# The first network of a hybrid decoder in block products, the last pair too, and the reciprocal root on VectorE

## The chip, the cores and the metric

One core of one Trainium2 chip runs the whole program. The metric is the device time of one execution in microseconds (us); lower is better. TensorE multiplies (PE in the views), VectorE is DVE, ScalarE is ACT, GpSimd is POOL, SyncE is SP.

## The reference

Two decoder layers work on 512 prompt tokens and 32 sample tokens (544 columns) of width 1024. Each layer has a gated network, a mixing stage and a second gated network:

```python
def swiglu(x, w_up, w_down):
    a, u = jnp.split(x @ w_up, 2, axis=-1)
    return (jax.nn.silu(a) * u) @ w_down

x = layer_norm(ALPHA * x + 0.5 * swiglu(x, p['ffn1_up'], p['ffn1_down']), p['ln1_g'], p['ln1_b'])
proj = x @ p['w_in'] + p['b_in']          # q, k, v, glu, gates
...                                       # window attention and causal convolution
c = jax.nn.silu(layer_norm(c, p['conv_ln_g'], p['conv_ln_b']))
mix = (jax.nn.sigmoid(g_attn) * (attn @ p['w_attn_out'])
       + jax.nn.sigmoid(g_conv) * (c @ p['w_conv_out']))
x = layer_norm(ALPHA * x + mix @ p['w_out'], p['ln2_g'], p['ln2_b'])
x = layer_norm(ALPHA * x + 0.5 * swiglu(x, p['ffn2_up'], p['ffn2_down']), p['ln3_g'], p['ln3_b'])
```

The inner width of the gated networks is 2816 = 11 x 256. All is float32.

## The kernel before

Activations lie with their features on the partitions and the 544 tokens along the columns, in four pieces of 256 features (a pair of 128). The columns are worked in two halves of 272, called hf 0 and hf 1. Every float32 product is made of three passes over operands that are split into a high and a low part (`split`: a cast on ScalarE, L460, and a subtraction on VectorE, L461); weights are split by `prep`-like steps in the same way (L291 on ScalarE, L292 on VectorE).

A standard unit (`unit`, L451 to L453) multiplies 256 output columns by one half of the tokens: 8 x 2 x 3 = 48 matmuls. An up pair j of a network is two weights, "a" for the gate and "u" for the value, so four units; `silu` applies the activation on ScalarE (L605) and `gated` the multiplication on VectorE (L611). The last unit of a layer's network is a down unit (`down_unit`, L717 adds its result).

Three of the four networks make the pairs j = 2 to 9 as block products instead (`up_fast`): each block of 128 columns is one 2 x 2 product by seven multiplications, which `product` (L664) does in 12 matmuls each, and one preparing matmul (L678). The left factors are differences of weight blocks (L312, L322, L352), made by a planner (`fill`, `steps`), which hands work to VectorE and ScalarE piece by piece while TensorE's estimated time advances. The right factors T are differences of blocks of the activations (`right`, L568 to L574); they are made where the norm before the network writes its result (`ln_out`). The first layer's first network has no norm in front of it. There `residual` (L585, L586) makes the scaled tokens that the result is added to, and all its pairs are standard units, in groups of 3, 3, 3 and 2 (`GROUPS`), each followed by the down units of the group before. Pair 10 is made of standard units in every network.

At the end of a network (`tail`) the last down units run beside the layer norm of the two halves: `centre` sums over the features on TensorE (L482) and subtracts the mean (L487), `newton` sums the squares (L504) and calls `rsqrt`, and `scale` spreads the result over the columns on TensorE (L512) and multiplies (L516). `rsqrt` makes three small operations on VectorE (L526 to L528) and eleven on GpSimd (L530 to L540), in series. These norms stand in 14 places; the last one of the program works on rows instead and has two more chains (L893, L902).

`setup_layer` loads the layer's small vectors by DMAs on GpSimd's queue, turns them on TensorE (L992, L1001, L1012) and copies them out of PSUM on VectorE (L994, L1002, L1013). It runs after the first two pairs (`up_first`) of the layer's first network, in `mark`. Transposed late tokens are brought in between the units of `up_first` (`late`). Weights come by DMAs on SyncE's queue (L166, L172).

The order of instructions is that of the program, apart from down units and norm steps at a network's end and in the middle of a network, which are mixed by due times.

## Time and profile before

| what | value |
|---|---|
| median of 3 runs | 2626.16 us (2626.13 to 2630.38) |
| profiled execution, its own time | 2630.69 us |
| span of the profile | 2628.7 us |
| TensorE busy | 2552.5 us (97%) |
| VectorE busy | 1715.0 us (65%) |
| ScalarE busy | 1126.2 us (43%) |
| GpSimd busy | 298.0 us (11%) |
| granted TensorE clock, mean of the run | 0.981 |

The span is the part of an execution that the profile covers; 2.0 us of the profiled execution lie outside it. Busy time is the time in which an engine worked on an instruction. A clock of 1.00 is 2.4 GHz, and 0.50 is 1.2 GHz, the lower of the two levels.

### The profile page before, as it was taken

How to read it: one execution, taken by the hardware profiler on the slowest of the kernel's cores; microseconds unless marked ns; L12 is line 12 of the kernel's file. 1: busy time of each engine (PE TensorE's matmuls, PEld its weight loads, DVE VectorE, ACT ScalarE, POOL GpSimd, SP SyncE). 2: the span in 40 equal slices, each digit the busy share in tenths (PEclk: the TensorE clock that was granted, in tenths of full speed). 3: DMA queues.
4: the chain of work that ended last, by engine and by line, in shares of the span. 5: the costliest groups of instructions: out<-in, count | busy, mean ns of one | idle time of the engine just before them, and what ended most of it. 6: DMA issues, size and time to landing. Idle time of an engine off the chain costs nothing.

```text
span 2628.7 us, 47397 instructions
## 1 busy us (share of the span) xinstructions
PE 2552.5 (97%) x20110; PEld 2502.8 (95%) x20110; DVE 1715.0 (65%) x2567; ACT 1126.2 (43%) x1972; POOL 298.0 (11%) x499
## 2 busy tenths in 40 slices
PE   8999999999999999999989999989999999999996
PEld 7999999988999999999989999989899999999996
DVE  4333237797986567666556666549979766676645
ACT  4222124477526254443344443245773353444431
POOL 2000001722301000000020000017232000000001
PEclk8999999999999999999989999989999999999998
DMA  7223133231322213332422333312214222233331
GB/s 219 83 89 104 54 109 85 50 95 53 101 65 87 91 58 96 97 97 89 133 75 82 97 97 97 116 49 76 82 53 113 69 81 87 78 93 97 97 101 39
DMA packets 302628, 232.15 MB, mean 88 GB/s; under 512 B 43812, under 2 KB 300020, under 8 KB 302320
## 3 DMA queue, kind: packets, MB, share of 16 engines
q1 hardware_dynamic: 298576, 220.37, 27.8%
q0 software_dynamic: 3840, 8.76, 1.1%
q8 instruction: 157, 2.57, 0.4%
q14 instruction: 55, 0.45, 0.1%
HBM read 225.69 MB, written 9.16 MB: 89 GB/s over the span
## 4 chain that ended last, share of the span: by engine, by line
PE 82%; DVE 8%; POOL 4%; ACT 3%; issue 2%; DMA 1%; DVEq 0%; POOLq 0%; ACTq 0%
PE pa L453 20%; PE pa L451 20%; PE pa L452 20%; PE pa L664 11%; PE pb L664 8%; DVE pr L1126 3%; POOL f L1141 2%; DVE wl L292 1%; DVE pr L461 1%; PE pb L1266 1%; DVE at L1247 1%; PE pa L1237 1%; PE pb L1278 1%; ACT at L1251 1%; PE pb L512 0%
## 5 line engine op out<-in xcount | busy, mean ns | idle before, releaser
L451 PE MATMUL pa<-pr,wh 128*128 128x272 f32 (+1 forms) x4032 | 1176.1, 293 | 18.7 <-ACT pr L460 11.1
L453 PE MATMUL pa<-pr,wl 128*128 128x272 f32 (+1 forms) x4032 | 1173.4, 292 | 4.9 <-DVE wl L292 4.9
L452 PE MATMUL pa<-pr,wh 128*128 128x272 f32 (+1 forms) x4032 | 1170.3, 291 | 3.7 <-DVE pr L461 3.6
L451 PEld LDWEIGHTS pa<-pr,wh 128*128 128x128 f32 x4032 | 765.8, 190 | 26.0 <-ACT pr L460 13.5
L452 PEld LDWEIGHTS pa<-pr,wh 128*128 128x128 f32 x4032 | 771.5, 191 | 8.2 <-DVE pr L461 6.0
L453 PEld LDWEIGHTS pa<-pr,wl 128*128 128x128 f32 x4032 | 765.6, 190 | 6.1 <-DVE wl L292 5.7
L292 DVE TENSOR_TENSOR wl<-raw,wh 128x1024 fp32r<-128x1024 f32 (+1 forms) x268 | 309.8, 1183 | 77.3 <-ACT wh L291 54.0
L1126 DVE SCALAR_TENSOR_TENSOR pr<-u,cw,pr 128x512 f32<-128x512 f32 x480 | 344.4, 764 | 2.2 <-ACT pr L1119 2.0
L291 ACT CAST wh<-raw 128x1024 fp32r<-128x1024 f32 (+1 forms) x268 | 259.9, 1009 | 159.8 <-PE pa L453 90.9
L453 PE MATMUL pa<-pr,wd 128*128 128x272 f32 x768 | 221.8, 289 | 0.0
L451 PE MATMUL pa<-pr,wd 128*128 128x272 f32 x768 | 221.4, 288 | 0.0
L452 PE MATMUL pa<-pr,wd 128*128 128x272 f32 x768 | 220.8, 288 | 0.0
L717 DVE SCALAR_TENSOR_TENSOR pr<-pa,pr 128x544 f32<-128x544 f32 (+2 forms) x152 | 109.7, 722 | 153.5 <-PE pa L453 152.7
L530 POOL TENSOR_SCALAR nw<-nw 91x3 f32<-91x3 f32 (+2 forms) x16 | 5.6, 349 | 1703.2 <-DVE nw L526 1703.2
L460 ACT CAST pr<-f 128x544 fp32r<-128x544 f32 (+1 forms) x124 | 79.7, 647 | 216.4 <-DVE f L611 116.1
L664 PE MATMUL pa<-pr,wa 128*128 128x272 f32 x1152 | 160.9, 289 | 0.0
L664 PE MATMUL pb<-pr,ws 128*128 128x272 f32 x1152 | 159.6, 288 | 0.0
L664 PEld LDWEIGHTS pa<-pr,wa 128*128 128x128 f32 x1152 | 151.4, 188 | 0.0
L664 PEld LDWEIGHTS pb<-pr,ws 128*128 128x128 f32 x1152 | 150.0, 188 | 0.0
L452 PEld LDWEIGHTS pa<-pr,wd 128*128 128x128 f32 x768 | 145.1, 189 | 0.0
L451 PEld LDWEIGHTS pa<-pr,wd 128*128 128x128 f32 x768 | 144.5, 188 | 0.0
L453 PEld LDWEIGHTS pa<-pr,wd 128*128 128x128 f32 x768 | 144.3, 188 | 0.0
(225 smaller groups left out, 3139.6 us busy)
## 6 DMA issues: line engine op xcount, KB each, us to landing
raw<-in_ffn_up_dram SPq DMA_DIRECT2D x174, 512.0 KB, 4.4
raw<-in_ffn_down_dram SPq DMA_DIRECT2D x76, 512.0 KB, 3.6
raw<-in_w_in_dram SPq DMA_DIRECT2D x72, 512.0 KB, 4.1
raw<-in_w_in_dram SPq DMA_DIRECT2D x64, 128.0 KB, 3.0
raw<-in_w_attn_out_dram SPq DMA_DIRECT2D x32, 256.0 KB, 4.0
raw<-in_w_conv_out_dram SPq DMA_DIRECT2D x16, 512.0 KB, 3.4
raw<-in_w_out_dram SPq DMA_DIRECT2D x16, 512.0 KB, 4.3
raw<-in_ffn_down_dram SPq DMA_DIRECT2D x24, 256.0 KB, 2.8
```

What stands on the lines that cost most here:

```text
L291: ins = self.nc.scalar.copy(wh, t)
L292: self.nc.vector.tensor_tensor(wl, t, wh.bitcast(F32), op=ALU.subtract)
L451: pin(self.nc.tensor.matmul(o, lhsT=wh, rhs=h, start=k == 0, stop=False))
L452: pin(self.nc.tensor.matmul(o, lhsT=wh, rhs=lo, start=False, stop=False))
L453: pin(self.nc.tensor.matmul(o, lhsT=wl, rhs=h, start=False, stop=k == kk - 1))
L460: pin(self.nc.scalar.copy(hi, src))
L461: pin(self.nc.vector.tensor_tensor(lo, src, hi.bitcast(F32), op=ALU.subtract))
L664: mm = lambda a, b, first=False, last=False: pin(nc.tensor.matmul(o, lhsT=a, rhs=b, start=first, stop=last, skip_group_check=True))
L717: pin(nc.vector.scalar_tensor_tensor(Y[p][:, :, hs], ps, 0.5, Y[p][:, :, hs], op0=ALU.mult, op1=ALU.add))
L1126: self.last["cw"] = nc.vector.scalar_tensor_tensor(cc[:, m, 0:SEQ], u[:, m, k:k + SEQ], cw[:, 8 * k + c:8 * k + c + 1], cc[:, m, 0:SEQ], o ...
L1141: nc.gpsimd.tensor_tensor(pr[:, 4 * b:4 * b + 4, :], win, wv.unsqueeze(1).to_broadcast([128, DS, KC]), op=ALU.mult)
L1237: nc.tensor.matmul(s[:, 2 * r + t, :], lhsT=q, rhs=k, start=t == 0 and ps == 0, stop=ps == 2, skip_group_check=True)
```

## The change

Four things change.

1. The first layer's first network makes its pairs j = 2 to 9 as block products, as the others do. Its right factors are made by `first_right` from the raw tokens, in `up_first`, between the units of the second half. The function also adds the two parts of the tokens (y), which `scaled` then multiplies on ScalarE; `residual` is no longer called there.
2. Pair 10 is made as two blocks, s(10, 0) and s(10, 1), in all four networks; the weights of the last down group come through the planner.
3. The eleven operations of `rsqrt` that ran on GpSimd run on VectorE.
4. `setup_layer` issues its DMAs before `up_first`, and does the turning on TensorE in a function `turn` that is called behind `up_first`; the copies of the caches (`shift_caches`) follow it.

```diff
-        g = self.nc.gpsimd
+        g = self.nc.vector
         g.tensor_scalar_mul(u, v, RS_B * RS_B)
...
-        return o + [("a", 10), ("u", 10)] + [("dn", 4, p, 0) for p in range(4)]
+        return o + [s(10, 0), s(10, 1)] + [("dn", 4, p, 0) for p in range(4)]
...
-                    if hf and j and self.is_fast(l, f):
+                    if hf and j:
                         begin()
+                    elif hf and not Y0:
+                        first_right()
                     gated(ws[2 * j + 1], hs[j], hf, sa)
...
+        def first_right():
+
+            for xh, xl in X:
+                y = self.pair()
+                nc.vector.tensor_tensor(y, xh.bitcast(F32), xl.bitcast(F32), op=ALU.add)
+                Y0.append(y)
+                T.append(self.right(y)())
...
-            self.stop = self.pi + len(self.ffn_order(l, f)) - 10
+            self.stop = self.pi + len(self.ffn_order(l, f)) - 4
...
-            for kind, *k in self.fast_order()[4:-6]:
+            for kind, *k in self.fast_order()[4:-4]:
...
+        gl = len(GROUPF) - 1
+        turn = self.mark(l, f)
+        up_first()
+        Y += self.scaled(Y0)
+        turn()
+        middle()
+        if last:
+            self.cut = FB[FK[1][0]][0]
+        ws = []
+
+        def pre(hf):
+            if hf == 0:
+                ws.extend(self.V(l, f, "dn", gl, p) for p in range(4))
+            else:
+                self.ahead(A3)
...
-            if l == 0:
-                self.setup2()
-            self.setup_layer(l)
-            if l:
-                self.shift_caches(l)
+
+        if f != "ffn1":
+            return lambda: None
+        if l == 0:
+            self.setup2()
+        turn = self.setup_layer(l)
+
+        def rest():
+            turn()
+            self.shift_caches(l)
+        return rest
```

`right(y)` is the function that makes the factors: three differences on VectorE, a cast on ScalarE, and, when its result is called, the low part on VectorE.

**VectorE at the start.** In the rows of before, L611 multiplies a gated unit (f), L461 makes the low part of its split, L586 scales the tokens and L292 makes low parts of weights:

```order
L611 TENSOR_TENSOR f_397<-pa_416,f_397 128x544
L461 TENSOR_TENSOR pr_210<-f_397,pr_209 128x2x272
L586 SCALAR_TENSOR_TENSOR pr_674<-pr_87,pr_674 128x1088
L586 SCALAR_TENSOR_TENSOR pr_677<-pr_89,pr_677 128x1088
...
L586 SCALAR_TENSOR_TENSOR pr_683<-pr_93,pr_683 128x1088
L292 TENSOR_TENSOR wl_742<-raw_737,wh_741 128x1024
...
L611 TENSOR_TENSOR f_517<-pa_519,f_517 128x544
...
L461 TENSOR_TENSOR pr_208<-f_517,pr_207 128x2x272
...
L611 TENSOR_TENSOR f_620<-pa_622,f_620 128x544
L461 TENSOR_TENSOR pr_210<-f_620,pr_209 128x2x272
```

In the rows of the change, L592 and L442 are that multiplication and split, L620 is the addition, L549 to L555 are `right`, and L298 makes the low part of the first down weight (wd). The units are numbered up to the eighth, which is f_696:

```order
L592 TENSOR_TENSOR f_433<-pa_452,f_433 128x544
L442 TENSOR_TENSOR pr_246<-f_433,pr_245 128x2x272
L620 TENSOR_TENSOR pr_555<-pr_86,pr_87 128x1088
L549 TENSOR_TENSOR pr_557<-pr_555 128x544
L550 TENSOR_TENSOR pr_557<-pr_555,pr_557 128x272
...
L555 TENSOR_TENSOR pr_559<-pr_557,pr_558 128x1088
...
L620 TENSOR_TENSOR pr_585<-pr_92,pr_93 128x1088
...
L592 TENSOR_TENSOR f_696<-pa_733,f_696 128x544
...
L555 TENSOR_TENSOR pr_589<-pr_587,pr_588 128x1088
L442 TENSOR_TENSOR pr_246<-f_696,pr_245 128x2x272
L298 TENSOR_TENSOR wd_708<-raw_698,wd_707 128x1024
```

The four scalings have gone from VectorE, and 20 operations of `first_right` stand in their place; the eighth unit's split and the first down weight's low part stand behind them.

**TensorE at the end of the first network, first half.** In the rows of before, L504 are the sums of `newton`, L512 those of `scale`, and the rest are rows of down units:

```order
L504 MATMUL pb_3996<-ones,pr_3679 91x1 x3
L451 MATMUL pa_4105<-pr_3206,wh_3733 128x272
...
L453 MATMUL pa_4105<-pr_3206,wl_3734 128x272
...
L453 MATMUL pa_4131<-pr_3676,wl_3740 128x272
...
L453 MATMUL pa_4158<-pr_3206,wl_3746 128x272
L512 MATMUL pb_4042<-ident,nw_4001 128x91 x3
L451 MATMUL pa_4158<-pr_3676,wh_3745 128x272
```

In the rows of the change, L485 is `newton`, L493 is `scale`, and L463 is `centre` of the second half:

```order
L433 MATMUL pa_4376<-pr_3754,wd_4013 128x272
L434 MATMUL pa_4376<-pr_3753,wd_4014 128x272
L485 MATMUL pb_4277<-ones,pr_4004 91x1 x3
L493 MATMUL pb_4326<-ident,nw_4282 128x91 x3
L463 MATMUL pb_4461<-pr_4003,ones 128x272
L432 MATMUL pa_4435<-pr_86,wh_4176 128x272
```

Before, 51 rows of down units lie between the two steps; now the one follows the other. In the second half there are 84 rows between them now, and 44 before; at the second layer's first end 85, and 39 before.

**VectorE in the second half of the convolution's norm, first layer.** In the rows of before, L500 is the last sum of squares, L526 to L528 are VectorE's part of `rsqrt`; the splits L461 and the scalings L586 of the tokens follow:

```order
L500 TENSOR_TENSOR pr_8277<-pr_8277 128x272
L526 TENSOR_SCALAR nw_8657<-pb_8653 91x3
L527 TENSOR_SCALAR nw_8659<-nw_8657 91x3
L528 TENSOR_SCALAR nw_8658<-nw_8659 91x3
L461 TENSOR_TENSOR pr_8857<-pr_4717,pr_8856 128x2x272
...
L461 TENSOR_TENSOR pr_8875<-pr_7207,pr_8874 128x2x272
L586 SCALAR_TENSOR_TENSOR pr_8880<-pr_87,pr_8880 128x1088
```

In the rows of the change, L507 to L521 are `rsqrt`, L442 the splits and L567 the scalings:

```order
L481 TENSOR_TENSOR pr_8480<-pr_8480 128x272
L507 TENSOR_SCALAR nw_8860<-pb_8856 91x3
L508 TENSOR_SCALAR nw_8862<-nw_8860 91x3
...
L442 TENSOR_TENSOR pr_9060<-pr_4920,pr_9059 128x2x272
L513 TENSOR_TENSOR nw_8862<-nw_8862,nw_8860 91x3
...
L442 TENSOR_TENSOR pr_9078<-pr_7410,pr_9077 128x2x272
...
L518 TENSOR_SCALAR nw_8860<-nw_8862 91x3
L567 SCALAR_TENSOR_TENSOR pr_9083<-pr_87,pr_9083 128x1088
...
L521 TENSOR_TENSOR nw_8861<-nw_8861,nw_8860 91x3
L567 SCALAR_TENSOR_TENSOR pr_9092<-pr_93,pr_9092 128x1088
```

The fourteen operations of `rsqrt` now share the queue with four splits and three scalings. On TensorE 89 rows lie between `newton` and `scale` there, where 47 lay before.

## Rows read from the trace of the kernel before

**Rows 1.** The page: busy time and share; the chain that ended last.
```profile
PE 2552.5 (97%) x20110; PEld 2502.8 (95%) x20110; DVE 1715.0 (65%) x2567; ACT 1126.2 (43%) x1972; POOL 298.0 (11%) x499
...
PE 82%; DVE 8%; POOL 4%; ACT 3%; issue 2%; DMA 1%; DVEq 0%; POOLq 0%; ACTq 0%
```

**Rows 2.** Windows: span, busy us (count) PE, PEld, DVE, ACT, POOL; PEclk, DMA, GB/s.
```profile
60.00:395.00 335.00, 335.00 (x2666) 334.83 (x2665) 111.05 (x129) 76.51 (x96) 0.00 (x0) 1.00 0.29 91
395.00:470.00 75.00, 71.71 (x571) 70.78 (x570) 46.64 (x71) 34.56 (x56) 12.60 (x23) 1.00 0.28 75
960.00:1240.00 280.00, 280.00 (x2221) 280.00 (x2220) 195.58 (x256) 122.33 (x189) 0.00 (x0) 0.99 0.30 91
1295.00:1350.00 55.00, 45.21 (x324) 43.74 (x323) 35.16 (x56) 23.25 (x37) 9.85 (x32) 0.84 0.34 112
1690.00:1765.00 75.00, 64.78 (x483) 63.30 (x481) 41.33 (x64) 32.04 (x52) 7.85 (x23) 0.91 0.26 67
```

**Rows 3.** Groups by line and shape: busy us, mean ns, idle before, releaser.
```profile
L312 DVE TENSOR_TENSOR wd<-raw,wd 128x1024 fp32r<-128x1024 f32 x48 | 58.2, 1217 | 5.5 <-PE pa L664 2.9 <-ACT wd L322 2.6
...
L574 DVE TENSOR_TENSOR pr<-pr,pr 128x1088 fp32r<-128x1088 f32 x12 | 15.5, 1293 | 12.8 <-ACT pr L571 12.8
...
L568 DVE TENSOR_TENSOR pr<-pr 128x544 f32<-128x544 f32 x12 | 8.6, 717 | 0.0
...
L569 DVE TENSOR_TENSOR pr<-pr,pr 128x272 f32<-128x272 f32 x12 | 5.2, 437 | 0.2
```

**Rows 4.** The start, timeline (start, us, engine, what, idle before, releaser) and window.
```profile
50.73 0.72 DVE L461 TENSOR_TENSOR pr<-f,pr 128x544 fp32r<-128x544 f32 x1 [0.71 <-ACT pr L460]
51.74 4.90 DVE L586 SCALAR_TENSOR_TENSOR pr<-pr,pr 128x1088 f32<-128x1088 f32 x4 [0.29 <-ACT pr L585]
...
73.36 0.72 DVE L611 TENSOR_TENSOR f<-pa,f 128x544 f32<-128x544 f32 x1 [3.89 <-PE pa L453]
...
33.98 0.56 PE L451 MATMUL pa<-pr,wh 128*128 128x272 f32 x1 [4.22 <-DVE pr L461]
...
34.00:39.00 5.00, 5.00 (x23) 5.00 (x24) 2.57 (x6) 1.58 (x4) 0.00 (x0) 0.52 0.81 276
```

**Rows 5.** Timeline of a root's chain and scaling; two of layer two.
```profile
1315.84 0.16 DVE L527 TENSOR_SCALAR nw<-nw 91x3 int32<-91x3 int32 x1
...
1316.11 0.17 DVE L528 TENSOR_SCALAR nw<-nw 91x3 int32<-91x3 int32 x1
...
1318.84 0.19 POOL L540 TENSOR_TENSOR nw<-nw,nw 91x3 f32<-91x3 f32 x1
...
1319.08 1.58 PE L512 MATMUL pb<-ident,nw 91*128 91x91 f32 x6 [4.33 <-POOL nw L540]
...
1714.87 1.38 PE L512 MATMUL pb<-ident,nw 91*128 91x91 f32 x5 [4.54 <-POOL nw L540]
...
1739.48 0.79 PE L512 MATMUL pb<-ident,nw 91*128 91x91 f32 x5 [1.60 <-POOL nw L540]
```

**Rows 6.** Timeline of the convolution norm's second chain; a window behind it.
```profile
819.15 0.16 DVE L526 TENSOR_SCALAR nw<-pb 91x3 f32<-91x3 f32 x1 [1.10 <-PE pb L504]
...
822.54 1.23 POOL L535 TENSOR_TENSOR nw<-nw 91x3 f32<-91x3 f32 x1
...
827.07 1.40 PE L512 MATMUL pb<-ident,nw 91*128 91x91 f32 x6 [2.04 <-POOL nw L540]
...
827.00:832.00 5.00, 4.93 (x27) 4.93 (x28) 3.50 (x5) 4.97 (x9) 0.01 (x1) 0.66 0.00 0
```

**Rows 7.** Timeline of the second layer's setup; GpSimd's last early issue.
```profile
1381.64 0.38 PE L1012 MATMUL pb<-nw,f 4*128 4x4 f32 x2 [2.97 <-DVE vec L994]
...
24.16 0.55 POOL L1025 DMA_DIRECT2D out_new_conv_sample_dram<-in_state_conv_dram  x1
```

**Rows 8.** Timeline of VectorE at the end.
```profile
2613.96 2.47 DVE L893 SCALAR_TENSOR_TENSOR at<-at,mv,at 128x1024 f32<-128x1024 f32 x2
2618.76 2.74 DVE L902 SCALAR_TENSOR_TENSOR at<-at,nw,at 128x512 f32<-128x512 f32 x4 [2.32 <-POOL nw L540]
```

More of the change, by code (lines that the diff above doesn't have):

```diff
@@ L226, in plan @@
         self.tp = self.ta = self.td = 0.0
-    @staticmethod
-    def is_fast(l, f):
-        return (l, f) != (0, "ffn1")
     def ffn_order(self, l, f):
         o = []
-        if self.is_fast(l, f):
-            for kind, *k in self.fast_order():
-                if kind != "dn" or k[2] == 0:
-                    o.append((kind, *k[:2]))
-            return o
-        for g, n in enumerate(GROUPS):
-            for i in range(n):
-                o += [("a", 3 * g + i), ("u", 3 * g + i)]
-                if i == 0 and g > 0:
-                    o += [("dn", g - 1, p) for p in range(4)]
-        o += [("dn", len(GROUPS) - 1, p) for p in range(4)]
+        for kind, *k in self.fast_order():
+            if kind != "dn" or k[2] == 0:
+                o.append((kind, *k[:2]))
         return o
@@ L430, in W @@
         return ms, kk
-    def P(self, *key):
-        self.ahead(2)
-        return self.W(*key, la=1)
     def unit(self, w, xs, hf, pin=lambda i: i):
@@ L617, in new_h @@
             return h
-        def up(g, i):
-            j = 3 * g + i
-            w = self.W(l, f, "a", j, la=LAU if j < 9 else LAV)
-            sa = [silu(w, hf) for hf in range(2)]
-            w = self.W(l, f, "u", j, la=LAU if j < 9 else LAV)
-            h = new_h(g)
-            for hf in range(2):
-                gated(w, h, hf, sa[hf])
         def up_first():
@@ L717, in down_unit @@
             pin(nc.vector.scalar_tensor_tensor(Y[p][:, :, hs], ps, 0.5, Y[p][:, :, hs], op0=ALU.mult, op1=ALU.add))
-        def down(g, get=self.W):
-            for p in range(4):
-                w = get(l, f, "dn", g, p)
-                for hf in range(2):
-                    down_unit(w, g, p, hf)
-            del H[g]
         def middle():
@@ L990, in setup_layer @@
                             a["b_in"][l, DQ:].rearrange("(c p) -> c p", p=128))
[L991 to L995 removed]
         wr = a["conv_dw_w"][l].rearrange("k (c p) -> (k c) p", p=128)
[L997 removed]
+        wrows = self.f1(shape=[128, 2, 128])
         for h in range(2):
[L999 to L1001 removed]
@@ L1002, in setup_layer @@
-        self.after(nc.vector.tensor_copy(cw, ps[:, :248]), "cw")
+            nc.gpsimd.dma_start(wrows[:124, h, :], wr[124 * h:124 * h + 124, :])
         nsk = t([128, NH], F32, f"nsk{l}")
         nc.gpsimd.dma_start(nsk, a["attn_sinks"][l:l + 1, :].to_broadcast([128, NH]))
-        nc.vector.tensor_scalar_mul(nsk, nsk, -1.0)
-        nsks = t([128, 4], F32, f"nsks{l}")
-        sk4 = self.sp.tile([128, 4], F32, tag="nw", name=self.nm("nw"))
+        sk4 = self.sp.tile([128, 4], F32, tag="sk", name=self.nm("sk"))
@@ L1017, in setup_layer, with turn @@
-        self.cw.append(cw)
-        self.nsk.append(nsk)
-        self.nsks.append(nsks)
-        self.bv.append(bv)
+        def turn():
+            ps = self.p1()
+            nc.tensor.transpose(ps[:, :NVEC], rows[:NVEC, :], self.ident[:NVEC, :NVEC])
+            vec = t([128, NVEC], F32, f"vec{l}")
+            nc.vector.tensor_copy(vec, ps[:, :NVEC])
+            cw = t([128, KC * 8], F32, "cw")
+            ps = self.p1()
+            for h in range(2):
+                nc.tensor.transpose(ps[:, 124 * h:124 * h + 124], wrows[:124, h, :], self.ident[:124, :124])
+            self.after(nc.vector.tensor_copy(cw, ps[:, :248]), "cw")
+            nc.vector.tensor_scalar_mul(nsk, nsk, -1.0)
+            nsks = t([128, 4], F32, f"nsks{l}")
+            ps = self.p1()
+            nc.tensor.matmul(ps[:, :4], lhsT=sel, rhs=sk4[:4], start=True, stop=True)
+            nc.vector.tensor_copy(nsks, ps[:, :4])
+            self.vec.append(vec)
+            self.cw.append(cw)
+            self.nsk.append(nsk)
+            self.nsks.append(nsks)
+            self.bv.append(bv)
@@ L1022, in shift_caches @@
+        return turn
     def shift_caches(self, l):
```

68 lines of the change are left out of this document (2 added, 66 removed).

## The prediction

> **What bounds the kernel now.** I read the page first, then windows by stage, then the timeline around each gap of TensorE. TensorE is busy for 2552.5 of 2628.7 us and makes up 82% of the chain that ended last [rows 1], so the time is TensorE's matmuls, plus the few places where it stands. Between 60 and 395 us, in the first network, 2666 matmuls fill 335 us without a hole: 335/2666 = 0.1257 us for each [rows 2]. Block products are no dearer: 280/2221 = 0.1261 between 960 and 1240 us, in a network that has them [rows 2]. So I count matmuls at 0.1257 us and call what is left of a stretch its loss. At the end of the first network (395 to 470 us) that is 75 - 571 x 0.1257 = 3.2 us. At the ends of two networks that already work in blocks it is 55 - 324 x 0.1257 = 14.3 us (1295 to 1350) and 75 - 483 x 0.1257 = 14.3 us (1690 to 1765) [rows 2]. The reader is to see there that the networks in block products are gapless inside (280.00 of 280 us, VectorE busy for 195.58 of them) and lose time only at their ends.
>
> **Matmuls saved.** A pair of up columns as standard units is 4 units of 48 = 192 matmuls; as two blocks it is 2 x (7 x 12 + 1) = 170. Twelve pairs change: eight of the first network and the last pair of all four networks. 12 x 22 = 264 matmuls, and 264 x 0.1257 = **33.2 us** less. It holds in full only if no new block waits for its factors.
>
> **The start.** The right factors are made on VectorE between the up units of the first two pairs: for each of four pieces an addition, one difference of 0.72, two of 0.44, and the low part of 1.29 behind a ScalarE cast, for which VectorE idles 12.8/12 = 1.07 us [rows 3]. The addition of two 128x1088 tensors has no row; by the low part, of the same size and two inputs, it is 1.29. That makes 5.25 us a piece, 21.0 in all, in place of four scalings of 4.90 together [rows 4]. VectorE is free at 50.73 + 0.72 = 51.45 us. Three pieces (15.75), a multiplication and a split of a gated unit (1.44), and the fourth piece up to its cast (2.89) take it to 71.5. The eighth unit's product comes at 73.36 [rows 4]. Behind it stand, in VectorE's order, the multiplication (0.72), two small copies (0.6 by estimate: 272 columns take 0.44), the last low part (1.29), the split (0.72) and the first low part of a down weight (1.22): 77.9 us, and more if a ScalarE cast comes late [rows 3, 4]. TensorE, which before went straight on, wants this weight some 0.7 us after the unit, with only three small jobs ahead: it stands 4 us or a little more; I take 4.4. Then the clock: before, after a stand of 4.22 us, TensorE did 23 matmuls in 5 us at a granted clock of 0.52, the lower level, in place of 23 x 0.1257 = 2.9 us [rows 4]; 2.1 us more. Together **+6.5**; bounds 0 (VectorE has caught up) and 10 (a second wait behind it).
>
> **The first network's end.** Before, 51 rows of the down units lie between the norm's statistics and its scaling, and hide the reciprocal root. After, there are none in the first half, as in the other networks, whose ends lose 14.3 us. Less what the root's move gives there (below), 12.0, against 3.2 now: **+8.8**; bounds 0 and 11.1.
>
> **The root's chain.** Where nothing was beside it, the second of its 14 operations started at 1315.84 us and the last at 1318.84, and the scaling matmuls stood 4.33 us for it [rows 5]. A GpSimd operation there takes 0.19 us, but 1.23 while VectorE runs its long ones [rows 6]. On VectorE two dependent small operations start 0.27 us apart though each takes 0.17 [rows 5], so 14 of them take about 3.5 us: bare, the move is worth 0.2 us. What it gains is the stretching, and the cover that the new order puts before the scaling. In the convolution's norm the second chain ran from 819.15 until the scaling matmuls at 827.07, 7.9 us in place of 3.5; TensorE stood 2.04 us for it, and then did 27 matmuls in 5 us: 5 - 0.07 - 3.4 = 1.5 lost to the clock, 3.6 in all, twice [rows 6]. After, four splits (0.72) and three scalings (1.22) [rows 4] stand between its operations on VectorE: 3.5 + 2.9 + 3.7, less what overlaps about 9.5 us. But 89 rows of matmuls lie in the gap in place of 47, 11.2 us, so it is covered. I leave 1.0 each for what those rows no longer cover elsewhere: 2 x 2.6 = **-5.2**; bounds 0 and -7.2. At the second layer's first end the stand of 4.54 is for a stretched chain and becomes 0.7 shorter; the second, 1.60, gets 85 rows in place of 39 and goes [rows 5]: **-2.3**. The first layer's second network: **-0.2**. In the last norm the chain's first three operations (0.5 us) stood ahead of two long ones of VectorE, 2.47 us, and the scaling then waited 2.32 us for the rest on GpSimd [rows 8]; in series 3.5 + 2.5 takes the place of 0.5 + 4.8: **+0.7**, with the first of the two chains **+0.9**.
>
> The row that prices a small VectorE operation is weighed against a page. The Trainium skill, "VectorE: DVE Perf Modes", section "The TRN2 errata", gives a float32 tensor_tensor (N+151)/0.96 ns, 0.16 us here; by that figure alone, as an estimate, a chain would take 2.2 us and every exposed chain would give 1.3 more. The rows agree on the duration and not on the distance. The same page of the Trainium skill, section "The DRAIN you can't avoid" lets the next operation start only when the pipeline is empty: chained or not, so 11 operations more are 11 such distances; the trace agrees (0.27). On GpSimd's stretched rows the trace agrees with the Trainium skill, "SBUF — State Buffer", section "Who interferes with whom": a VectorE instruction with two SBUF inputs contends with GpSimd's reads.
>
> **Last pair and setup.** The two blocks of the last pair are prepared inside the blocks before them, and the last group's down weights follow inside the second. VectorE has 30% of its time free in such a stretch [rows 2]; I cost them at nothing. If the second block were late, that is a few us in each of four networks (a rival, below). At the second layer's setup TensorE stood 2.97 us behind a copy from PSUM that weight operations held up on VectorE [rows 7]; in the new order the copy comes directly: about 1.1 left, **-1.9**. The setup's small DMAs move ahead of the first units, and the cache copies behind them. They are on GpSimd's queue, which before had issued them all by 24.7 us and then idled [rows 7]; what they bring is wanted at 74 us, so neither they nor what they pass costs anything.
>
> **Sum.** -33.2 + 6.5 + 8.8 - 5.2 - 2.3 - 0.2 + 0.9 - 1.9 = **-26.6 us**. The profiled execution had 2630.7, which gives 2604.1. It lies 4.5 above the median of 2626.2, which gives **2600**.
>
> **Rivals.**
> - *The ends and the start stay hidden.* VectorE catches up in the start, and the first network's end loses no more than now: -33.2 - 9.6 + 0.9 = -41.9, 2584. For it speaks that VectorE is idle in pieces of 4 us in the start [rows 4]; against it, the orders.
> - *VectorE's queue is late in more places.* The norms keep their stands (0 in place of -5.2), the start costs 10, the end 11.1: -26.6 + 5.2 + 3.5 + 2.3 = -15.6, 2611. For it: eleven operations in 16 chains now wait their turn among operations of 0.7 to 1.3 us, in an order fixed beforehand.
> - *The root is cheaper than I count.* If the operations followed each other at their own 0.17 us [rows 5], a chain would take 2.4 us, and six exposed ends (the first halves of three networks, the last norm's two chains and one more) would give 1.1 each: -33.2, 2593. Against it stands the distance of 0.27 between two VectorE rows. The formula of the Trainium skill, "VectorE: DVE Perf Modes", "The TRN2 errata", would make it so.
> - *The other side: blocks wait for VectorE.* Each of 24 new blocks adds splits and differences to VectorE. If each made TensorE wait 26.6/24 = 1.1 us, nothing would be left; at 1.5 us the time would be 2626.2 - 26.6 + 36 = 2636. Against it stands the gapless stretch of 280 us with the same blocks [rows 2]. In the first network VectorE has nothing more to do than there.
>
> **How the numbers follow.** The forecast has 0.48, with a range of its own of 2593 to 2606. Hidden start and ends: 0.12. Late queue: 0.24. Cheap root: 0.09. Blocks that wait: 0.07, of which half is on the wrong side of no change. 0.2% is 5.3 us, about what can be told here. Faster 0.91, same 0.05, slower 0.04. The range, 2586 to 2614, takes in the cheap root and the late queue, and leaves out the two outer cases.
>
> **What would show it.** TensorE's matmuls: 264 fewer. In 60 to 400 us no gap. A stand of 4 to 5 us near 74 us with the lower clock behind it; if there is none, the first rival holds. At the first network's end a stand of about 4 us before the scaling matmuls in its first half. No stand before the scaling in the second half of the convolution's norm; if it is there with VectorE as releaser, the late queue is right. Wrong altogether if the blocks of the first network show waits for VectorE, or the loss at its end is well over 14 us.

## The result, and the profile after

The changed kernel takes 2599.26 us (median of 5 runs) against 2630.38 for the kernel before on the same chip: a ratio of 0.9888, 95% interval 0.9872 to 0.9904. Four of its runs lie between 2594.78 and 2602.92; the fifth took 3064.55 at a mean granted clock of 0.745, where the others had 0.934 to 0.982, and is left out of the ratio. The forecast of 2600 and its range held. The change itself was forecast as -26.6 and came as -31.1 by the medians: the level was met because the median of three runs before, from which it was taken, lay 4.2 us below that of five. The profiled execution took 2602.92 us with a span of 2600.8; the span is 27.9 us shorter than before.

The page of the changed kernel: busy time of each engine, then the chain that ended last.

```profile
PE 2522.6 (97%) x19846; PEld 2471.7 (95%) x19846; DVE 1882.3 (72%) x2955; ACT 1195.6 (46%) x2116; POOL 238.7 (9%) x323
...
PE 84%; DVE 8%; ACT 4%; POOL 2%; issue 1%; DMA 0%; DVEq 0%; ACTq 0%; POOLq 0%
```

Against [rows 1] TensorE has 20110 - 19846 = 264 matmuls fewer, exactly the number forecast. VectorE works 167 us more and is no bound.

Windows of the changed kernel (columns as in [rows 2]): the first network, its end, the two other ends, then three short stretches.

```profile
60.00:360.00 300.00, 296.36 (x2341) 295.63 (x2340) 211.50 (x277) 127.77 (x200) 0.00 (x0) 0.99 0.31 93
360.00:440.00 80.00, 72.02 (x547) 70.62 (x547) 53.56 (x98) 35.91 (x57) 0.15 (x1) 0.91 0.37 105
1275.00:1330.00 55.00, 46.04 (x334) 44.59 (x333) 40.15 (x81) 25.30 (x41) 0.00 (x0) 0.88 0.22 68
1665.00:1740.00 75.00, 67.08 (x507) 65.68 (x507) 44.28 (x86) 32.49 (x53) 0.14 (x1) 0.91 0.25 67
73.00:78.00 5.00, 4.56 (x19) 4.24 (x20) 4.93 (x6) 2.22 (x3) 0.00 (x0) 0.50 0.55 156
404.00:414.00 10.00, 4.70 (x16) 3.64 (x17) 7.47 (x17) 6.43 (x13) 0.00 (x0) 0.50 0.00 0
818.00:823.00 5.00, 4.86 (x26) 4.86 (x27) 3.63 (x6) 5.00 (x10) 0.00 (x0) 0.66 0.03 8
```

At the first network's end 80 - 547 x 0.1257 = 11.2 us are lost now, 3.2 before [rows 2]. The first row's hole of 3.6 us lies in the start, and the fifth row shows the lower clock behind it.

The start, timelines of VectorE and of TensorE, changed kernel (columns as in [rows 4]).

```profile
69.17 0.72 DVE L592 TENSOR_TENSOR f<-pa,f 128x544 f32<-128x544 f32 x1
...
70.25 1.29 DVE L555 TENSOR_TENSOR pr<-pr,pr 128x1088 fp32r<-128x1088 f32 x1
71.79 0.72 DVE L442 TENSOR_TENSOR pr<-f,pr 128x544 fp32r<-128x544 f32 x1 [0.25 <-ACT pr L441]
72.74 2.36 DVE L298 TENSOR_TENSOR wd<-raw,wd 128x1024 fp32r<-128x1024 f32 x2 [0.22 <-ACT wd L308]
...
72.76 0.60 PE L432 MATMUL pa<-pr,wd 128*128 128x272 f32 x1 [3.21 <-ACT wd L308]
74.02 0.60 PE L434 MATMUL pa<-pr,wd 128*128 128x272 f32 x1 [0.44 <-DVE wd L298]
```

The eighth unit's multiplication (L592) comes at 69.17, 4.2 us earlier than in [rows 4], and the stand of 3.2 and 0.4 us that was forecast comes right behind it.

The first network's end and the convolution's norm, TensorE's timeline of the changed kernel: the scaling behind the root, the first unit behind it, and the first unit behind the second half of the convolution's norm.

```profile
405.22 1.56 PE L493 MATMUL pb<-ident,nw 91*128 91x91 f32 x6 [3.75 <-DVE nw L521]
...
410.28 0.82 PE L432 MATMUL pa<-pr,wh 128*128 128x272 f32 x2 [2.54 <-ACT pr L441]
...
818.14 0.52 PE L432 MATMUL pa<-pr,wh 128*128 128x272 f32 x2 [2.85 <-ACT pr L441]
```

In the convolution's norm the stand before the scaling [rows 6] is gone; one of 2.85 us stands behind it.

To see where the rest of the time went I cut the span at the same marks in each profile and take, for each stage, its time less that in the first profile of before, less 0.1257 us for each matmul more or less (us; negative is shorter). "Again" is a second execution of the kernel before (an experiment below).

| stage | again | changed | root_gpsimd | right_early | conv_gpsimd | best |
|---|---|---|---|---|---|---|
| start, to the eighth unit | -0.1 | -4.2 | -7.0 | -6.4 | -6.4 | -6.0 |
| eighth unit to the first mix | 0.0 | 13.1 | 18.3 | 7.2 | 11.9 | 7.2 |
| first mix | -3.2 | -1.3 | -2.1 | -1.3 | -2.6 | -2.0 |
| convolution's norm, layer 1 | -1.0 | 1.9 | -1.0 | 2.8 | 0.0 | -0.1 |
| its second network, with its end | -2.1 | -2.6 | -2.4 | -2.7 | -2.8 | -2.7 |
| layer 2, setup and first network | 1.5 | -2.2 | -2.1 | -2.1 | -2.1 | -2.1 |
| that network's end | 0.4 | -3.5 | 0.0 | -3.6 | -3.5 | -3.6 |
| second mix | 1.5 | 5.0 | 1.3 | 2.2 | 2.2 | 2.1 |
| convolution's norm, layer 2 | 1.6 | 2.9 | 1.5 | 1.9 | -1.0 | -1.0 |
| last network and last norm | 0.4 | -3.1 | 0.2 | -2.9 | -3.2 | -3.1 |

The column "again" tells what one execution can: the same program differs by up to 3.2 us in a mix and by up to 2.1 elsewhere. At the start it differs by 0.1 there, but root_gpsimd and conv_gpsimd, which have the changed kernel's program up to the eighth unit, reach it 2.8 and 2.2 us sooner than it did in its profile.

### The profile page after: what moved, and what is told of

Its sections match the earlier page's. It is cut to its first block, busy times and chain, and to the rows that moved or that the text cites. A ratio compares the mean times of both kernels' runs of the same rounds, so it can differ in the third digit from the quotient of the medians.

```text
span 2600.8 us, 47137 instructions
## 1 busy us (share of the span) xinstructions
PE 2522.6 (97%) x19846; PEld 2471.7 (95%) x19846; DVE 1882.3 (72%) x2955; ACT 1195.6 (46%) x2116; POOL 238.7 (9%) x323
## 3 DMA queue, kind: packets, MB, share of 16 engines
q8 instruction: 155, 2.54, 0.4%
## 4 chain that ended last, share of the span: by engine, by line
PE 84%; DVE 8%; ACT 4%; POOL 2%; issue 1%; DMA 0%; DVEq 0%; ACTq 0%; POOLq 0%
PE pa L646 17%; PE pa L434 17%; PE pa L432 17%; PE pa L433 17%; PE pb L646 12%; DVE pr L1075 3%; POOL f L1090 2%; DVE wl L278 1%; PE pa L1186 1%; PE pb L1215 1%; PE pb L1227 1%; DVE pr L442 1%; DVE pr L497 1%; PE pb L493 0%; ACT pr L1426 0%
## 5 line engine op out<-in xcount | busy, mean ns | idle before, releaser
L432 PE MATMUL pa<-pr,wh 128*128 128x272 f32 x2624 | 770.0, 295 | 24.0 <-ACT pr L441 18.5
L434 PE MATMUL pa<-pr,wl 128*128 128x272 f32 x2624 | 768.9, 294 | 6.2 <-DVE wl L278 6.2
L433 PE MATMUL pa<-pr,wh 128*128 128x272 f32 x2624 | 766.5, 293 | 5.8 <-DVE pr L442 5.8
L432 PEld LDWEIGHTS pa<-pr,wh 128*128 128x128 f32 x2624 | 502.2, 192 | 31.5 <-ACT pr L441 21.7
L433 PEld LDWEIGHTS pa<-pr,wh 128*128 128x128 f32 x2624 | 506.0, 193 | 10.6 <-DVE pr L442 8.2
L434 PEld LDWEIGHTS pa<-pr,wl 128*128 128x128 f32 x2624 | 502.8, 192 | 7.2 <-DVE wl L278 7.0
L432 PE MATMUL pa<-pr,wd 128*128 128x272 f32 (+2 forms) x1408 | 406.0, 289 | 3.2 <-ACT wd L308 3.2
L434 PE MATMUL pa<-pr,wd 128*128 128x272 f32 (+2 forms) x1408 | 408.1, 290 | 0.4 <-DVE wd L298 0.4
L433 PE MATMUL pa<-pr,wd 128*128 128x272 f32 (+2 forms) x1408 | 405.6, 288 | 0.0
L1075 DVE SCALAR_TENSOR_TENSOR pr<-u,cw,pr 128x512 f32<-128x512 f32 x480 | 349.5, 779 | 1.9 <-ACT pr L1068 1.7
L432 PEld LDWEIGHTS pa<-pr,wd 128*128 128x128 f32 x1408 | 265.5, 189 | 3.4 <-ACT wd L308 3.3
L433 PEld LDWEIGHTS pa<-pr,wd 128*128 128x128 f32 x1408 | 267.2, 190 | 0.0
L434 PEld LDWEIGHTS pa<-pr,wd 128*128 128x128 f32 x1408 | 265.5, 189 | 0.9 <-DVE wd L298 0.8
L646 PE MATMUL pa<-pr,wa 128*128 128x272 f32 x1728 | 241.4, 289 | 0.0
L278 DVE TENSOR_TENSOR wl<-raw,wh 128x1024 fp32r<-128x1024 f32 x168 | 204.8, 1238 | 34.4 <-ACT wh L277 33.8
L277 ACT CAST wh<-raw 128x1024 fp32r<-128x1024 f32 x168 | 170.9, 1047 | 93.7 <-PE pa L433 41.9
L699 DVE SCALAR_TENSOR_TENSOR pr<-pa,pr 128x544 f32<-128x544 f32 (+2 forms) x160 | 115.3, 723 | 133.0 <-PE pa L434 131.4
L664 ACT COPY pb<-pa 128x272 f32<-128x272 f32 x72 | 26.6, 370 | 295.9 <-PE pa L646 295.9
L442 DVE TENSOR_TENSOR pr<-f,pr 128x544 fp32r<-128x544 f32 x124 | 89.2, 723 | 83.1 <-ACT pr L441 83.0
```

What stands on the lines that cost most here:

```text
L277: ins = self.nc.scalar.copy(wh, t)
L278: self.nc.vector.tensor_tensor(wl, t, wh.bitcast(F32), op=ALU.subtract)
L432: pin(self.nc.tensor.matmul(o, lhsT=wh, rhs=h, start=k == 0, stop=False))
L433: pin(self.nc.tensor.matmul(o, lhsT=wh, rhs=lo, start=False, stop=False))
L434: pin(self.nc.tensor.matmul(o, lhsT=wl, rhs=h, start=False, stop=k == kk - 1))
L442: pin(self.nc.vector.tensor_tensor(lo, src, hi.bitcast(F32), op=ALU.subtract))
```

## The experiments

All times are medians, with the ratio to the kernel before on the same chip. The runs were made on several chips, so two of them are compared by their ratios; differences of medians are given beside that. "Changed" is the kernel under study.

| run | us | ratio, 95% interval |
|---|---|---|
| changed | 2599.26 | 0.9888, 0.9872 to 0.9904 |
| root_gpsimd | 2604.18 | 0.9904, 0.9891 to 0.9917 |
| last_std | 2603.81 | 0.9903, 0.9891 to 0.9916 |
| first_std | 2615.98 | 0.9947, 0.9933 to 0.9961 |
| setup_late | 2618.70 | 0.9953, 0.9936 to 0.9970 |
| chain_first | 2612.74 | 0.9937, 0.9925 to 0.9949 |
| chain_first2 | 2598.83 | 0.9885, 0.9866 to 0.9903 |
| right_early | 2591.76 | 0.9852, 0.9834 to 0.9870 |
| conv_gpsimd | 2595.45 | 0.9866, 0.9846 to 0.9886 |
| best | 2585.74 | 0.9832, 0.9818 to 0.9845 |
| warm | 2593.33 | 0.9860, 0.9847 to 0.9874 |
| best_warm | 2583.07 | 0.9821, 0.9808 to 0.9835 |

**The root back on GpSimd (root_gpsimd).**

```diff
-        g = self.nc.vector
+        g = self.nc.gpsimd
```

> The changed kernel with the eleven operations of the root back on GpSimd. Theory A, the term of the prediction: the move gave 6.8 us, so this runs at about 2606 (ratio to before 0.991), and in the convolution's norms TensorE stands 2 us ahead of the scaling again. Theory B, from the profile after: in the convolution's norms the move gave nothing, since the stand went from before the scaling to behind it, and only the two ends and the last norm gained; then this runs 1 to 4 us above the changed kernel, 2600 to 2603.

By the medians the move is worth some 4 to 5 us, but the intervals overlap. The stages say where: without it the first network loses 5.2 more up to the mix (its scalings wait 4.45 and 2.11 us, in the changed kernel 3.75 and not at all), the second layer's first end 3.5 and the last norm 3.3, and the two norms of the convolution are 4.3 better. Most of the last norm's gain is not the chain's length but what stands behind it. VectorE's timeline of the kernel before (its second execution), then TensorE's of root_gpsimd, then VectorE's and TensorE's of the changed kernel:

```profile
2604.99 4.05 DVE L902 SCALAR_TENSOR_TENSOR at<-at,nw,at 128x512 f32<-128x512 f32 x6 [1.55 <-POOL nw L540]
2608.98 0.67 DVE L717 SCALAR_TENSOR_TENSOR pr<-pa,pr 128x512 f32<-128x512 f32 x1
```

```profile
2584.33 0.66 PE L822 MATMUL pa<-ident,pr 128*128 128x128 f32 x4 [3.07 <-DVE pr L699]
```

```profile
2582.89 0.69 DVE L699 SCALAR_TENSOR_TENSOR pr<-pa,pr 128x512 f32<-128x512 f32 x1 [1.06 <-PE pa L434]
2583.50 4.04 DVE L846 SCALAR_TENSOR_TENSOR at<-at,nw,at 128x512 f32<-128x512 f32 x6
...
2583.64 0.66 PE L822 MATMUL pa<-ident,pr 128*128 128x128 f32 x4 [0.35 <-DVE pr L699]
```

With GpSimd's root the six scalings wait 1.55 us at the head of VectorE's queue and then run for 4.05, and the last down unit's addition (L717, L699 after), for which TensorE waits, stands behind them: TensorE waits 3.07 us. With VectorE's root the addition stands ahead of them and TensorE waits 0.35. The kernel before waits 3.09 and 3.08 us there in its two profiles.

**The last pair as standard units, as before (last_std).**

```diff
-        return o + [s(10, 0), s(10, 1)] + [("dn", 4, p, 0) for p in range(4)]
+        return o + [("a", 10), ("u", 10)] + [("dn", 4, p, 0) for p in range(4)]
...
+        wa = self.P(l, f, "a", 10)
...
+        gated(wu, h, 1, sa[1])
```

> The changed kernel with the last pair as standard units in all four networks, as before. 4 x 22 = 88 matmuls more, 11.1 us at 0.1257 us each. Theory A: the blocks of the last pair wait for nothing, so the whole 11 us comes back, 2610 (ratio 0.993). Theory B: they cost waits on VectorE that the profile spreads over the ends, and only about half comes back, 2605.

It costs 4.6 us by the medians where 4 x 22 matmuls are 11.1, and the intervals overlap. Its profile has the 88 matmuls more, and gives them back in stages that have no last pair: the start and the two mixes are 8.6 us shorter than the changed kernel's, the convolution's norms 4.0. That is what single executions differ by, so what the two blocks cost at the four ends can't be read from it. Half explained.

**The first network as standard units, the other parts kept (first_std).** The first network's units, its `residual` and its end are as before: 198 matmuls more than in the changed kernel (nine pairs), or 24.9 us. In short:

```diff
+    def is_fast(l, f):
+        return (l, f) != (0, "ffn1")
```

> The changed kernel with the first layer's first network in standard units, as before. 9 x 22 = 198 matmuls more: +24.9. The stand for the first down weight and the low clock behind it go: -5.6. The end of that network is covered again: -8.0. Theory A, the start of the changed kernel is 4.2 us earlier because of the order of its first weights: the eighth unit's multiplication on VectorE is back at about 73.4 us, and the time is 2599 + 24.9 - 13.6 + 4.2 = 2614. Theory B, the earlier start was chance in when weights landed: it stays at about 69.2, or lies anywhere between, and the time is about 2610.

It is 16.7 us slower by the medians, a little more than either theory gave: of the 24.9 us of matmuls 8.9 come back between the eighth unit and the mix, where 4.1 us are lost in place of 13.1. The start didn't go back to 73.3 us, though: the eighth unit came at 67.0. So the start's gain is not that of the block products.

**The setup behind the units (setup_late).**

```diff
-        turn = self.mark(l, f)
         up_first()
         Y += self.scaled(Y0)
-        turn()
+        self.mark(l, f)()
```

> The changed kernel with the setup of the layers as before: its DMAs issued behind the first units. Theory A: the earlier start of the changed kernel (the eighth unit at 66 to 69 us in five profiles, 73.3 in the one of before) comes from this, and the stand at the second layer's setup (2.97 before, 1.02 now) comes back with it: eighth unit at about 73, and 4 to 7 + 1.9 us more, 2606. Theory B: the start is chance in when weights land: eighth unit at 66 to 69, and only the 1.9 us, 2601.

The issue of the setup's DMAs and the turning stand behind the units again, and the time rises by 19 us. Timelines of setup_late: GpSimd's queue, then TensorE. Behind them, GpSimd's queue of the kernel before with the same copy.

```profile
7.81 0.59 POOL L973 DMA_DIRECT2D out_new_k_sample_dram<-in_cache_k_dram  x1
8.39 0.56 POOL L973 DMA_DIRECT2D out_new_v_sample_dram<-in_cache_v_dram  x1
...
25.21 1.94 PE L888 MATMUL pa<-ident,at 128*128 128x128 f32 x8 [5.61 <-DMA at<-in_x_prompt_dram]
...
40.66 0.57 PE L432 MATMUL pa<-pr,wh 128*128 128x272 f32 x1 [4.23 <-DVE pr L442]
...
90.24 0.58 PE L961 MATMUL pb<-sk,f 4*128 4x4 f32 x2 [9.81 <-DVE vec L952]
```

```profile
22.98 0.61 POOL L1025 DMA_DIRECT2D out_new_k_sample_dram<-in_cache_k_dram  x1
```

The 4.23 at 40.66 is the stand of before [rows 4]; the other two are in neither the changed kernel nor the kernel before. The cache copies, 992 KB each, are issued at 7.8 us here, at 20.7 in the changed kernel and at 23.0 in the kernel before, where the setup's DMAs stand ahead of them. The tokens' 448 KB take 18.9 us to land here, 9.6 and 13.3 there; that the early copies are the reason is argued from these times. And `turn`'s copy from PSUM, called behind `first_right`, waits until VectorE has worked off the factors and the first down weights: 9.8 us. So the 19 us are the price of an order that neither kernel has, and not what part 4 gained over the kernel before. The stand at the second layer's setup is back as before: 2.98 us, in the changed kernel 1.02.

**The root's chain ahead of the splits and scalings (chain_first, chain_first2).** Both pin the convolution norm's second chain into one piece; the second also pins the first SiLU and the residual's scalings on ScalarE, so that the activation tables aren't changed back and forth. chain_first:

```diff
+            steps = self.ln_fin(acc, cl, hf, c_out)
+            if hf:
+                steps[2:2] = [(0.0, lambda: cut(0, keep))]
+            self.put_off(steps)
...
+            keep(nc.vector.scalar_tensor_tensor(y, xl.bitcast(F32), ALPHA, y, op0=ALU.mult, op1=ALU.add))
```

> The changed kernel with the convolution norm's second chain kept together on VectorE: the splits of the first half stand behind its last operation, and the four scalings behind the norm. Theory A: what the norms lose there (2.4 us each more than before) is the interleaving, which makes the chain 7.8 us long; uninterrupted it takes about 2.7, the scaling comes some 5 us earlier, the wait behind it falls from 2.85 us to 1.3 or less and the low clock goes: 3 to 4 us for each of the two norms, 2592. Theory B: the wait behind the scaling is set by what follows it (multiplications, activation, split), which is as long as before: within 1 us of the changed kernel.

> As chain_first, but ScalarE's order is held too: the first activation of the norm stands behind the last sigmoid, and the scaling of the tokens for the residual behind the splits. In chain_first the chain took 2.4 us and the scaling came without a stand, but ScalarE then loaded its activation table five times and did four scalings of 1.03 us ahead of the split that TensorE waited for. Theory A: the latency from the statistics to the first split is what the norm loses, and its parts are the interleaved chain (5 us) and ScalarE's order; with both in hand the wait of 2.85 us and the low clock behind it go, 4 us for each norm: 2591 (ratio 0.9855). Theory B: something else sets it, and the time is that of the changed kernel within 2 us, or worse.

ScalarE's timeline of chain_first, and TensorE's first unit behind the norm there:

```profile
806.29 1.12 ACT L1426 ACTIVATE pr<-pr,vec 128x272 f32<-128x272 f32 x2 [4.16 <-DVE pr L497]
807.43 1.28 ACT L1352 ACT_TABLE_LOAD   x1
808.72 0.49 ACT L1352 ACTIVATE pr<-pa,vec 128x272 f32<-128x272 f32 x1
809.22 1.28 ACT L1426 ACT_TABLE_LOAD   x1
810.51 1.12 ACT L1426 ACTIVATE pr<-pr,vec 128x272 f32<-128x272 f32 x2
811.65 1.28 ACT L1352 ACT_TABLE_LOAD   x1
...
814.07 4.11 ACT L1456 ACTIVATE pr<-pr 128x1088 f32<-128x1088 f32 x4
...
822.13 0.82 PE L432 MATMUL pa<-pr,wh 128*128 128x272 f32 x2 [6.73 <-ACT pr L1436]
```

The chain took 2.4 us in one piece and the scaling came without a stand, yet the first unit waited 6.73 us: the sigmoids now stand between the SiLUs, each change loads a table for 1.28 us (five loads there, one in the changed kernel), and the four scalings of 4.11 us come ahead of the split. In chain_first2 the stand before the first unit shrinks to 0.59, and the residual's scalings, put later, make the next weight's low part late: 2.42 us. It takes what the changed kernel takes: with the chain in one piece and ScalarE's order held the stand goes, and another comes in its place. A shorter chain alone wins nothing here.

**The factors one turn earlier (right_early).** The loop of `first_right` starts when the last delayed token step is done, in the first half of the units.

```diff
-                    elif hf and not Y0:
+                    elif not self.late and not Y0:
```

> The changed kernel with the right factors of the first network made one unit earlier, as soon as the last late tokens are in (at 41 us instead of 47). Theory A: the first down weight is late (a stand of 3.2 us, 0.4 behind it, and 2.2 us to the low clock) because its split stands behind the factors in VectorE's queue; with 6 us more room the stand goes, -5.8 us: 2593. Theory B: the stand is set by the weight's arrival or ScalarE's cast; no more than 1 us goes.

The stand at the start is gone. A window of right_early; the changed kernel has 149 matmuls in the same 25 us, at a granted clock of 0.86:

```profile
60.00:85.00 25.00, 25.00 (x200) 24.81 (x199) 19.70 (x27) 11.29 (x17) 0.00 (x0) 1.00 0.35 105
```

From the eighth unit to the mix it is 5.9 us shorter (4.7 beside conv_gpsimd, which has the changed kernel's program there), and `first_right`'s additions run from 37.28 us instead of 47.25.

**The convolution norm's root on GpSimd (conv_gpsimd).** `ln_fin` takes the engine of the root as an argument, and the two norms of the convolution pass GpSimd.

```diff
-            self.put_off(self.ln_fin(acc, cl, hf, c_out))
+            self.put_off(self.ln_fin(acc, cl, hf, c_out, nc.gpsimd))
```

> The changed kernel with the root on GpSimd in the convolution's norms alone, on VectorE everywhere else. Theory A, from the two profiles: the convolution's norms are the only place where the move lost (2.9 and 1.4 us against the kernel with the root on GpSimd), so this gains about 4 us: 2595. Theory B, the losses there are an effect of the order that comes out of the program, not of the engine: no change within 2 us.

By the medians it gains 3.8 us, but the intervals overlap; by the stages the two norms take 1.9 and 3.9 us less than in the changed kernel. TensorE's timeline of conv_gpsimd: the only stand there is that of [rows 6].

```profile
805.01 0.90 PE L493 MATMUL pb<-ident,nw 91*128 91x91 f32 x6 [2.04 <-POOL nw L521]
```

The timelines count the cover. In the changed kernel 89 matmuls lie between `newton` and the scaling, and 5 between the scaling and the first unit that needs the norm; in conv_gpsimd, as in the kernel before, they are 47 and 46. About as many matmuls as before hide the norm, but they have gone from behind the scaling to ahead of it.

What the changed kernel lost there has two parts. Its stand of 2.85 us (with one of 0.89 ahead of `newton`'s sums) is also in last_std, whose two norms nevertheless lose only 0.4 each. Windows of 25 us that begin 5.1 us before the stand ends, in the changed kernel and in last_std:

```profile
813.04:838.04 25.00, 22.16 (x165) 21.93 (x164) 17.18 (x23) 11.97 (x19) 0.00 (x0) 0.93 0.27 86
```

```profile
810.84:835.84 25.00, 22.15 (x177) 21.93 (x176) 18.66 (x24) 11.99 (x20) 0.00 (x0) 1.00 0.34 107
```

The same stand is followed by a granted clock of 0.93 over the window in one and 1.00 in the other: 12 matmuls, 1.5 us. So the stand itself costs 0.4 us against the first profile of before, and the clock the rest, in the executions in which it falls.

**Both edits that gained (best).** right_early and conv_gpsimd together.

> The changed kernel with both edits that gained alone: the residual right factors of both halves of the first network are made right behind its setup in every unit's turn (right_early), and the two layers' convolution norms keep their root on GpSimd while the networks' norms take VectorE's (conv_gpsimd). Theory A, the two waits are apart in the program and their gains add: from the changed kernel's 2599.3 us, the first network's start and end give back 5.9 (13.1 beyond its matmuls became 7.2) and the two convolution norms 5.7 (+1.86 and +2.91 became -0.01 and -0.96), so 2587 to 2588, ratio about 0.984. Theory B, a part of what each gained was the second layer's mix, which took 4.95 us beyond its matmuls in the changed kernel and 2.2 in both others, and can be won once only: 2590 to 2592, ratio about 0.985 to 0.986.

2585.74 us: the gains add, as the first theory said. By the medians it is 13.5 us below the changed kernel, and the intervals of the ratio don't meet.

**Filler matmuls against the low clock (warm, best_warm).**

```diff
+        def spin(ps, c, k):
+            for _ in range(k):
+                self.tc.keep_in_program_order(nc.tensor.matmul(
+                    ps[:, c:c + 128], lhsT=self.ident, rhs=self.ident, start=True, stop=True,
+                    skip_group_check=True))
...
+            if warm and not hf:
+                spin(ps, 128, 13)
```

> The changed kernel with filler matmuls that nothing reads (the identity by itself, 128 x 128 columns): 13 between the Newton step and the scaling of the first half's norm and 7 behind the centring of the second half's, at the ends of the three networks that another network or mix follows, 60 in all. Theory A, a good part of each end's loss is the low clock that the waits bring (half speed over some 13 to 14 us at the first network's end costs half of that, about 6.8 us, and about 2.5 at the two others), and keeping TensorE at work keeps the clock: the ends lose 5 and twice 1 to 2 us less, 2590 to 2593 us. Theory B, the ends are set by the chain of VectorE and ScalarE that the waits stand for, with the low clock hidden inside them: the time stays within 2 us of 2599.3. Theory C, the fillers' 60 x 0.06 us at full clock and the order that they force stand on the path themselves: 2601 to 2605 us.

> The same filler matmuls in the kernel with both gaining edits (best). By theory A of the fillers it is 5 to 8 us below best, by B within 2 us of it, by C 2 to 6 us above it. It also repeats best's two edits in another order of instructions, so that a gain that both show belongs to the edits.

Each filler shows as two matmul records, 120 in all. The first network's end and the 5 us behind its waits, best and then best_warm:

```profile
385.00:425.00 40.00, 32.17 (x225) 31.02 (x224) 26.91 (x61) 17.75 (x28) 0.15 (x1) 0.83 0.22 56
405.00:410.00 5.00, 5.00 (x24) 5.00 (x24) 4.02 (x7) 2.84 (x6) 0.00 (x0) 0.51 0.00 0
```

```profile
385.00:425.00 40.00, 36.12 (x279) 35.38 (x278) 29.14 (x65) 17.86 (x28) 0.15 (x1) 0.96 0.30 72
405.00:410.00 5.00, 5.00 (x30) 5.00 (x29) 3.68 (x6) 2.12 (x4) 0.00 (x0) 0.66 0.00 0
```

Over the 40 us the clock rises from 0.83 to 0.96, and of 279 matmuls 40 are fillers: 239 against 225 real ones, 14 x 0.1257 = 1.8 us gained where the first theory has 5. The clock isn't kept throughout: two waits of 1.46 and 1.83 us stay open behind the fillers, and in the 5 us behind them it is 0.66 (0.51 in best). At the two other ends the stages of warm are 1.7 longer and 1.1 shorter than the changed kernel's, those of best_warm 0.6 and 0.3 shorter than best's. So the runs show that a part of the low stretch lies under waits (in best 2.54 and 1.53 us of it), but not what the whole of it costs; nor is the fillers' own price, the third theory, told apart. The Trainium skill, "TensorE: Matmul & The Clock Gate", section "HAM oscillation — how this bites in real kernels", prices a throttled stretch at its time by (1 - 1.2/2.4); the trace doesn't agree for the whole of such a stretch here, since in those 4.1 us TensorE stands at either level. The median of warm alone, 5.9 us below the changed kernel, looked like the first theory; by stages its three ends give 0.5 of it, and the rest is in the mixes, the convolution's norms and the start, where no filler is. best_warm and best can't be told apart.

**The kernel before again (before_again).** One execution: 2629.35 us.

> The kernel before, unchanged. Theory A, the start up to the eighth unit, 73.3 us in the kernel before and 66.1 to 69.2 in the changed kernel and in its variants with the setup in front, is a property of the program: it is again 73 to 74 us here. Theory B, it is the hazard of when the first transfers land in one execution: it is anywhere from 66 to 74 us, and then the 4.2 us that the changed kernel won at its start are not the change's.

The eighth unit comes at 73.25 us, in the first profile at 73.36, and at 66.1 to 69.3 in all profiles with the setup in front: the earlier start is the program's and not chance. ScalarE's timeline of this execution, and of the changed kernel:

```profile
22.54 1.05 ACT L291 CAST wh<-raw 128x1024 fp32r<-128x1024 f32 x1 [4.93 <-DMA raw<-in_ffn_up_dram]
...
27.06 1.28 ACT L605 ACT_TABLE_LOAD   x1
28.35 0.62 ACT L605 ACTIVATE f<-pa 128x544 f32<-128x544 f32 x1
...
29.81 0.38 ACT L460 CAST pr<-pa 128x256 fp32r<-128x256 f32 x1
```

```profile
18.93 1.05 ACT L277 CAST wh<-raw 128x1024 fp32r<-128x1024 f32 x1 [4.75 <-DMA raw<-in_ffn_up_dram]
...
23.30 1.28 ACT L586 ACT_TABLE_LOAD   x1
24.59 0.62 ACT L586 ACTIVATE f<-pa 128x544 f32<-128x544 f32 x1
26.05 0.38 ACT L441 CAST pr<-pa 128x256 fp32r<-128x256 f32 x1
```

ScalarE's order is the same in both: casts of weights, the table, the first SiLU, the late tokens' splits. What differs is when a weight is there: its cast starts at 22.54 and at 18.93 us, and what follows is 3.8 us earlier with it; TensorE's stand behind these splits is 4.22 us before [rows 4] and 2.28 after. Every profile with the setup in front has this cast at 17.8 to 19.5 us, with the first network in standard units (first_std) and with the root on GpSimd too. So the gain goes with part 4. That part 4 alone brings it, and by which of its moved instructions, isn't shown: setup_late has the 4.23 again, but the cache copies stand in its way.

## Why the prediction was right, and where only its sum was

- **Matmuls saved (-33.2).** Right: 264 fewer, gapless inside.
- **The start (+6.5).** Right in place and size: 3.2 and 0.4 us of stand, 19 matmuls in the next 5 us at a clock of 0.50, and 4.7 to 5.9 us back when the factors came earlier. Missing was a term for the start ahead of it, -4.2 in this profile and up to -7.0 in others: "Last pair and setup" costs what is moved there at nothing.
- **The first network's end (+8.8).** Right: 7.2 us remain when the start's stand is away, with 3.75 us before the scaling where "about 4" was said.
- **The convolution's norms (-5.2).** Wrong in sign: +4.8 in the profile, +0.8 where the clock didn't fall. The chain took 7.8 us (802.75 to 810.53) instead of 9.5 and the scaling had no stand, as forecast. The step that failed is "I leave 1.0 each for what those rows no longer cover elsewhere". The 89 rows that went ahead of the scaling left 5 behind it in place of 46, where scaling, SiLU and split are in series; TensorE stood there 2.85 us instead. conv_gpsimd showed it. The rival of the late queue named a stand before the scaling as its sign, and there was none.
- **The last norm (+0.9).** Wrong in sign: -3.1. I counted the chain and not whose place behind it in VectorE's queue TensorE waits for; root_gpsimd showed the 3.07.
- **The second layer's first end (-2.3)** measured -3.5; the stand of its setup (-1.9) went from 2.97 to 1.02 us as forecast, and the stage shows -2.2. But "neither they nor what they pass costs anything" doesn't hold for every order: in setup_late the same instructions, otherwise placed, cost 19 us.
- **Not in the sum:** the second mix, +5.0. One VectorE operation there (L1075) took 5.76 us where it mostly takes 0.7, and TensorE stood 3.85 us for a weight, where it stands 1.8 in most profiles. The operation lasts as long as a run of GpSimd operations beside it (timelines below): thirteen in 6.36 us, 0.49 each, where they take 0.83 on average. In right_early, in the same place, VectorE's operation takes 0.93 us and twelve of GpSimd's take 9.13. Three other profiles have one such operation, 5.79 us (first_std) and 6.90 (chain_first, warm), and each ends 0.55 to 0.57 us after such a run. Why it comes in some executions and not in others is open.

GpSimd's run and VectorE's operation in the second mix, changed kernel:

```profile
1945.66 6.36 POOL L1090 TENSOR_TENSOR f<-f,cw 128x124 f32<-128x124 f32 x13
...
1946.82 5.76 DVE L1075 SCALAR_TENSOR_TENSOR pr<-u,cw,pr 128x512 f32<-128x512 f32 x1
```

The root's operations follow each other at 0.20 us, not 0.27, so the bare chain takes 2.6 us where I had 3.5; and the prediction's distance for every further operation, chained or not, holds only for chained ones: between long independent operations a small one cost the queue 0.07 us. With 2.6 us the rival of the cheap root (2.4) had the price nearly right, but that didn't decide the time. The Trainium skill, "VectorE: DVE Perf Modes", section "The TRN2 errata", by whose figure a chain was estimated at 2.2 us, lies nearer to the trace than my distance from one pair of rows did.

VectorE's timeline of the last norm's chain, changed kernel:

```profile
2589.64 0.16 DVE L512 TENSOR_TENSOR nw<-nw 128x2 f32<-128x2 f32 x1
2589.83 0.16 DVE L513 TENSOR_TENSOR nw<-nw,nw 128x2 f32<-128x2 f32 x1
2590.03 0.17 DVE L514 TENSOR_SCALAR nw<-nw 128x2 f32<-128x2 f32 x1
```

So the total came out right by luck: misses of -4.2 (start), -4.0 (last norm) and -7.4 (the smaller ones together) met +10.0 at the convolution's norms and +5.0 in the second mix, beside the three large terms that held. The level of 2600 had a second piece of luck: with the median of five runs before, 2630.38, the same sum gives 2603.8.

## What to carry to other kernels

Cover is spent once: matmuls that are moved ahead of one wait are missing behind it, so follow the chain up to the next operand that TensorE needs, not to the first. When a chain changes its engine, look at what stands behind its last operation in the new and the old queue; here that was worth more than the chain's own length. And before a total is taken to confirm a mechanism, compare the stages with a second execution of the same program: warm gave the forecast time for another reason.

## What was not expected of the hardware

- Dependent VectorE operations of 0.16 us on 128x2 operands start 0.20 us apart; one that stands between long independent ones costs the queue 0.07 us (804.06 to 804.13, 806.55 to 806.63).
- The same stand of 2.85 us was followed by a fall of the granted clock in some executions and not in others (0.93 and 1.00 over the same 25 us).
- Five table loads of 1.28 us in place of one stood in chain_first's way, though its chain was 5.4 us shorter.
- Where copies of 992 KB were issued on GpSimd's queue at 7.8 us, the tokens took 18.9 us to land; where they were issued at 20.7 us, 9.6.
- A VectorE operation of 0.7 us lasted 5.8 to 6.9 us beside a run of GpSimd operations, once each in 4 of 14 profiles.
